# TensorE's order fixed in pieces through the memory heads and the S5 stage, with two float32 products of S5 dropped

## Chip, cores and metric

One core of one Trainium2 chip (trn2). The metric is the device time of one execution in microseconds; the time before is the median of three runs.

## What is computed

A decoder trunk of two layers over 1024 positions and 1024 channels, batch 1, float32. Layer 0 mixes tokens with a gated DeltaNet (GDN, 8 heads), layer 1 with an S5 state-space layer (64 groups of 16 channels, each driving one complex state of 64). Beside each mixer runs a cross-attention with 4 heads into 256 memory tokens. Cut to what matters here:

```python
def s5_scan(u, abar, bbar, c):                    # h_t = Abar h_{t-1} + Bbar u_t ; y_t = Re(C h_t)
    ...
    y = einsum('cbgp,gip->bcgi', st_re, c_re) - einsum('cbgp,gip->bcgi', st_im, c_im)

def s5_mixer(x, ...):
    u, xq = jnp.split(x @ w_in, [S5_DIM], axis=-1)
    y = s5_scan(u, ...) + d_skip * u
    zg = jax.nn.gelu(y)
    return zg * jax.nn.sigmoid(zg @ w_glu + b_glu), xq

def memory_attention(xq, mem, w_kv):
    k, v = jnp.split(mem @ w_kv, 2, axis=-1)
    s = einsum('blhd,bmhd->bhlm', q, k) * (XA_HEAD_DIM ** -0.5)
    return einsum('bhlm,bmhd->blhd', softmax(s), v)

for i in range(2):
    mix, xq = gdn_mixer(x, ...) if i == 0 else s5_mixer(x, ...)
    h = concat([mix, memory_attention(xq, mem, w_kv_mem[i])]) @ w_o[i]
    x = layer_norm(ALPHA * x + h, ...)
    x = layer_norm(ALPHA * x + square(relu(x @ mlp_w1[i])) @ mlp_w2[i], ...)
```

## The kernel before

**Arithmetic.** The large products run as three float32r matmuls each: an operand is split into a high and a low half (`load_split`: ScalarE casts the high half, VectorE subtracts to get the low one), and `mm3` (lines 115 to 117) adds high x high, high x low and low x high in one PSUM bank. `proj_half` is one 128-row projection of one half (512 positions): 8 blocks of three matmuls 128x512. Products of the S5 core and the chunk stage run in plain float32, which shows as two records a product. The activations of a layer stand in SBUF as `xT` (two halves, high and low).

**Order.** The kernel is written in program order, and the framework's planner then orders each engine's instructions: by priority in program order, by its own estimates of durations, and by when a rotating buffer becomes free. All engines then run their queues strictly in the order planned. `behind(mark)` adds edges without semaphores from each instruction traced inside it to a marked one on the same engine, so it only fixes order within an engine; before the change it serves only the S5 setup (`s5_side`).

**Buffers.** SBUF tags have fixed counts (`TAGS`: h1 7, h2 9, h3 7, h4 6, h5 5, w1 4, raw 2, xT 6), PSUM banks too (`BANKS`: mm 2, pa 3, pi 1, po 1, sc 1). Weight tiles come through the two `raw` buffers on SP's queue (SyncE issues most DMAs).

**Stages in order of time.** First the input and the keys of two GDN heads (`gdn_a`), the inverse of their small blocks on GpSimd (`gdn_inverse`), and the memory keys and values (`mem_kv`). Then the four memory heads (`attend`), the keys of a third GDN head between the first and the second. Then the chunk stage (`gdn_b`, eight heads), the output projection, the first MLP (`mlp`), beside which `s5_side` builds S5's tables: per core m of 8 and half b of 2, `s5_mats` forms H1 (and its ninth power H8), a Toeplitz source Z, G1 and H2, and stores them to HBM. Then the S5 stage, GLU, output projection and second MLP.

**`attend`** (lines 777 to 823) for one head: the query projection of both halves (tile `wq`), then per half two score tiles `sc` in the banks pi and pa, softmax (line 800 maximum, 804 exponential, 807 scaling), transposes `pT` (line 813) into po and sc, split, and the value product `pv`.

**`s5_core(m)`** (lines 1122 to 1174). SP loads u, the Toeplitz matrix M0 (from `zd`, one buffer for all cores) and per half G1, two tables `tab`, H1 and H2. G2 is G1 with its column halves swapped, by two ScalarE copies (1149, 1150). Four products G1 x u (line 1152) and four G2 x u (1154) give the drive and its partner; VectorE multiplies each by a table (1157, 1158), adds (1159), scans along the positions (1162) and makes r1 (1165), while GpSimd makes r2 (1166). The read-out adds for each group M0 x u (1169), H1 x r1 (1170) and H2 x r2 (1171) in one bank, then GELU (1173) and a store to `yd`. `s5_u(m)` is the projection (tile `wu`) that gives core m its input; it stands ahead of the core before it, and after odd cores comes one memory head. `glu` reads `yd` back, splits it and projects (tile `wg`).

Of the kernel before, what the change touches and what calls it, by code (L numbers as in the profile page):

```python
# [28 lines left out]
class Trunk:  # L29
    def __init__(self, ctx, tc, a):  # L30
        self.tc = tc
        self.nc = nc = tc.nc
        self.a = a
        self.uid = 0
        self.turn = 0
        self.proj = 0
        self.cp = ctx.enter_context(tc.tile_pool(name="cp", bufs=1))
# [22 lines left out]
    def behind(self, mark):  # L60
# [716 lines left out]
    def attend(self, src, xT, kv, h, permute, tag):  # L777

        nc = self.nc
        kh, kl, vh, vl = kv  # L780
        scale = P ** -0.5
        q = [None, None]

        def evac(hf, ps):
            hi = self.tile("h4", [P, HALF], F32R, "qh")
            lo = self.tile("h3", [P, HALF], F32R, "ql")
            nc.scalar.copy(hi, ps)
            nc.vector.tensor_tensor(lo, ps, f32(hi), op=ALU.subtract)
            q[hf] = (hi, lo)

        self.proj_fm(src, xT, evac, "wq")
        for hf in range(2):
            pp = []
            for c in range(2):
                ps = self.psum(("pi", "pa")[c], "sc", (P, 2, 256))
                for j in range(2):
                    t = slice((2 * c + j) * P, (2 * c + j + 1) * P)
                    self.mm3(ps[:, j, :], (q[hf][0][:, t], q[hf][1][:, t]), (kh[:, h, :], kl[:, h, :]), True, True)
                mx = self.tile("st", [P, 6], F32, "mx")
                nc.vector.tensor_reduce(mx[:, 0:2], ps, axis=AX.X, op=ALU.max)  # L800
                nc.vector.tensor_scalar(mx[:, 0:2], mx[:, 0:2], -scale, None, op0=ALU.mult)
                p = self.tile(tag, [P, 2, 256], F32, "p")
                for j in range(2):
                    nc.scalar.activation(p[:, j, :], ps[:, j, :], AF.Exp, bias=mx[:, j:j + 1], scale=scale, accum_out=mx[:, 2 + j:3 + j])
                nc.vector.reciprocal(mx[:, 4:6], mx[:, 2:4])
                for j in range(2):
                    nc.vector.tensor_scalar(p[:, j, :], p[:, j, :], mx[:, 4 + j:5 + j], None, op0=ALU.mult)
                pp.append(p)
            pt = []
            for m in range(2):  # L810
                ps = self.psum(("po", "sc")[m], "pT")
                for t in range(4):
                    nc.tensor.transpose(ps[:, t * P:(t + 1) * P], pp[t // 2][:, t % 2, m * P:(m + 1) * P], self.ident)
                hi = self.tile(tag, [P, HALF], F32R, "pTh")
                lo = self.tile(tag, [P, HALF], F32R, "pTl")
                nc.scalar.copy(hi, ps)
                nc.vector.tensor_tensor(lo, ps, f32(hi), op=ALU.subtract)
                pt.append((hi, lo))
            ps = self.psum("mm", "pv")
            d = slice(h * P, (h + 1) * P)  # L820
            for m in range(2):
                self.mm3(ps, (vh[:, m, d], vl[:, m, d]), pt[m], m == 0, m == 1)
            self.keep_rows(8 + h, hf, ps, permute)
# [69 lines left out]
    def s5_scratch(self):  # L893
# [3 lines left out]
        self.h2d = d("h2d", [8, P, 8, P])  # L897
# [143 lines left out]
    def combine(self, eng, x, y, pr, pi, op, b, nm, tag="h5"):  # L1041

        n = pr.shape[1]
# [6 lines left out]
        eng.tensor_tensor(o, o, w, op=op)  # L1050
        return o

    def s5_coeffs(self, m):
# [6 lines left out]
        co = self.tile("gb", [P, 6, 8, 16], F32, "co")  # L1060
        x = self.tile("h5", [P, 3, 8, 16], F32, "s5b")
        for o, n in ((x[:, 0], "b1"), (x[:, 1], "b2"), (co[:, 5], "c1"), (co[:, 3], "c2")):
# [4 lines left out]
        V.tensor_scalar(co[:, 2], co[:, 5], self.sg, -1.0, op0=M, op1=M)  # L1067
        V.tensor_scalar(co[:, 4], co[:, 3], self.sg, None, op0=M)
# [9 lines left out]
    def s5_mats(self, m, b, co):  # L1078
# [3 lines left out]
        A_, S_ = ALU.add, ALU.subtract  # L1082
# [3 lines left out]
        h1 = self.combine(V, co[:, 2], co[:, 3], re[:, 0:8, gl], im[:, 0:8, gl], A_, b, "H1")  # L1086
        nc.gpsimd.dma_start(self.h1d[m, :, gs, 0:8], h1)
        h8 = self.combine(V, co[:, 2], co[:, 3], re[:, 8:9, gl], im[:, 8:9, gl], A_, b, "H8", "S")
# [9 lines left out]
        g1 = self.combine(V, co[:, 0], co[:, 1], re[:, 0:8, gl], im[:, 0:8, gl], A_, b, "G1T")  # L1098
# [6 lines left out]
        h2 = self.combine(V, co[:, 4], co[:, 5], re[:, 1:9, gl], im[:, 1:9, gl], S_, b, "H2")  # L1105
        nc.gpsimd.dma_start(self.h2d[m, :, gs], h2.rearrange("p g e o -> p g (e o)"))
# [15 lines left out]
    def s5_core(self, m):  # L1122

        nc = self.nc
        V, G = nc.vector, nc.gpsimd
# [3 lines left out]
        M0 = self.s5t[:, T:2 * T].rearrange("p (g x) -> p g x", g=8)  # L1129
        z = self.zd[m]  # L1130
        nc.sync.dma_start(M0, bass.AP(z.tensor, z.offset, [[16, 8], [8 * 240, 16], [240, 8], [1, P]]))
        for b in range(2):
# [3 lines left out]
            def load(tag, nm, src):  # L1136
                t = self.tile(tag, [P, 4, P], F32, nm)
                nc.sync.dma_start(t, src)
# [5 lines left out]
            H2 = load("h2", "H2", self.h2d[m, :, gs])  # L1144

            p1 = self.psum("pa", "p1", (P, 4, P))
            p2 = self.psum("pa", "p2", (P, 4, P))
            G2 = self.tile("h1", [P, 4, P], F32, "G2")
            nc.scalar.copy(G2[:, :, 0:64], G1[:, :, 64:128])
            nc.scalar.copy(G2[:, :, 64:128], G1[:, :, 0:64])  # L1150
            for g in range(4):
                nc.tensor.matmul(p1[:, g, :], G1[:, g], u[:, 4 * b + g, :], start=True, stop=True)
            for g in range(4):
                nc.tensor.matmul(p2[:, g, :], G2[:, g], u[:, 4 * b + g, :], start=True, stop=True)
# [5 lines left out]
            w = self.tile("h3", [P, 4, P], F32, "wsc")  # L1160
            for g in range(4):
                V.tensor_tensor_scan(w[:, g, :], self.r8[:, g0 + g:g0 + g + 1].to_broadcast([P, P]), t1[:, g, :], 0.0, M, A_)
            r1 = self.tile("h1", [P, 4, P], F32, "r1")
            r2 = self.tile("h1", [P, 4, P], F32, "r2")
            V.tensor_tensor(r1, w, tab[0], op=M)
            G.tensor_tensor(r2, w, tab[1], op=M)
            py = self.psum("pi", "py", (P, 4, P))
            for g in range(4):
                nc.tensor.matmul(py[:, g, :], M0[:, 4 * b + g, :], u[:, 4 * b + g, :], start=True, stop=False)
                nc.tensor.matmul(py[:, g, 1:], H1[:, g], r1[:, g, 0:P - 1], start=False, stop=False)  # L1170
                nc.tensor.matmul(py[:, g, 1:], H2[:, g], r2[:, g, 0:P - 1], start=False, stop=True)  # L1171
            zg = self.tile("h3", [P, 4, P], F32, "zg")
            nc.scalar.activation(zg, py, AF.Gelu_apprx_tanh)
            nc.sync.dma_start(self.yd[m].rearrange("s (o g) n -> (s o) g n", o=16)[:, gs, :], zg)
# [9 lines left out]
    def glu(self):  # L1184
        nc = self.nc
        zT = self.new_xT()
# [8 lines left out]
        bg = self.const("bglu", [P, 8])  # L1195
        nc.sync.dma_start(bg, self.a["bglu"])
        for m in range(8):
            def evac(hf, ps):
                sg = self.tile("h3", [P, HALF], F32, "sig")
                nc.scalar.activation(sg, ps, AF.Sigmoid, bias=bg[:, m:m + 1])  # L1200
                z = self.tile("h4", [P, HALF], F32, "zz")
                nc.gpsimd.tensor_tensor(z, f32(zT[hf][0][:, m, :]), f32(zT[hf][1][:, m, :]), op=ALU.add)
                nc.vector.tensor_tensor(sg, sg, z, op=ALU.mult)
                nc.sync.dma_start(self.cat[m * P:(m + 1) * P, hf * HALF:(hf + 1) * HALF], sg)

            self.proj_fm(self.a["w_glu"][m], zT, evac, "wg")


    def run(self):
# [17 lines left out]
        att = lambda h: self.attend(a["w_in"][32 + h], xT, kv, h, True, "h2")  # L1227
# [4 lines left out]
        att(0)  # L1232
        keys_of(2)
        att(1)
        att(2)
        att(3)
# [25 lines left out]
        for m in range(8):  # L1262
            if 0 < m < 7:
                for _ in self.s5_u(m + 1, xT):
                    pass
            self.s5_core(m)
            if m % 2:
                self.attend(a["w_in5"][8 + m // 2], xT, kv, m // 2, False, "h5")
        self.glu()
# [130 lines left out]
```

## Time and profile before

| | us |
|---|---|
| median of 3 runs (3015.02 to 3018.07) | 3017.49 |
| profiled execution | 3012.86 |
| its span, first to last instruction | 3010.8 |
| memory heads of layer 0, 76.7 to 216.1 | 139.4 |
| chunk stage, 216.1 to 870 | 653.9 |
| S5 stage with heads and GLU, 1775 to 2165.2 | 390.2 |

A row of a table of stretches gives the stretch, its length, the busy time of each engine in it with the count of instructions, the granted TensorE clock (1.00 is full), the share of the DMA engines and GB/s. PE is TensorE's matmuls, PEld its weight loads, DVE VectorE, ACT ScalarE, POOL GpSimd; SPq is SyncE's queue. A row of waits reads "engine line waited for: us in total, times, longest". A row of groups reads line, engine, operation, output and inputs, shapes, count, busy us, mean ns, idle before and what ended it. Ends of matmuls are modelled, and consecutive ones overlap.

### The profile page before, as it was taken

To read this page: it belongs to the slowest core of one execution; us is meant where nothing else is said; L and a number is where in the kernel's file an instruction comes from. 1 tells how busy PE (TensorE), PEld (TensorE's weight loads), DVE (VectorE), ACT (ScalarE), POOL (GpSimd) and SP (SyncE) were. 2 spreads that over 40 slices of the span, in tenths; PEclk is the share of its full clock that TensorE was granted. 3 is DMA by queue.
4 is the path that set the end of the run, shared out by engine and by line. 5 is a ranking of instruction groups with operands and counts; after the bars stand their busy time and mean duration, and the time that the engine had idled before them with its cause. 6 is when DMAs were issued, how large, how long until landed. Compare 5 with 4: busy or idle time off the path is not lost. (4 is left out here: it accounts for less than half of the span.)

```text
span 3010.8 us, 36564 instructions
## 1 busy us (share of the span) xinstructions
PE 2832.7 (94%) x13629; PEld 2297.6 (76%) x13629; DVE 1765.6 (59%) x3491; ACT 964.1 (32%) x2069; POOL 517.2 (17%) x745
## 2 busy tenths in 40 slices
PE   8789888898999999999999998987999999999998
PEld 6668776676788888777777877775888888888887
DVE  7735667665679687666665644444378444444346
ACT  5334444453422322222222222223222222322221
POOL 3620543716002021211110101012002000000002
PEclk9889999999999999999999999997999999999999
DMA  5322433423532232322222165555341111111111
GB/s 196 108 60 78 107 110 102 111 95 83 173 97 69 72 100 86 100 81 83 76 91 79 71 205 166 168 150 168 109 133 44 63 42 50 49 49 49 50 50 56
DMA packets 197490, 288.12 MB, mean 96 GB/s; under 512 B 86032, under 2 KB 119008, under 8 KB 197312
## 3 DMA queue, kind: packets, MB, share of 16 engines
q1 hardware_dynamic: 181696, 245.46, 26.2%
q0 software_dynamic: 13312, 36.13, 3.8%
q10 hardware_dynamic: 2304, 4.20, 0.4%
q8 instruction: 107, 1.75, 0.2%
q14 instruction: 71, 0.58, 0.1%
HBM read 213.93 MB, written 71.79 MB: 95 GB/s over the span
## 5 line engine op out<-in xcount | busy, mean ns | idle before, releaser
L252 DVE TENSOR_TENSOR y<-tm,y 128x512 f32<-128x512 f32 x448 | 307.8, 689 | 197.5 <-PE tm L117 193.8
L115 PE MATMUL w<-xTh,w1h 128*128 128x512 f32 x1024 | 401.7, 393 | 0.1
L116 PE MATMUL w<-xTl,w1h 128*128 128x512 f32 x1024 | 400.7, 391 | 0.0
L117 PE MATMUL w<-xTh,w1l 128*128 128x512 f32 x1024 | 400.1, 391 | 0.0
L115 PE MATMUL tm<-w2h,hh 128*128 128x512 f32 x1024 | 399.1, 390 | 0.0
L116 PE MATMUL tm<-w2l,hh 128*128 128x512 f32 x1024 | 398.1, 389 | 0.0
L117 PE MATMUL tm<-w2h,hl 128*128 128x512 f32 x1024 | 397.3, 389 | 0.0
L107 ACT CAST w2h<-w2r 128x512 fp32r<-128x512 f32 x128 | 76.4, 622 | 556.9 <-PE tm L117 441.9
L176 POOL TENSOR_SCALAR mv<-mv 128x1 f32<-128x1 f32 x32 | 40.5, 1266 | 1165.9 <-DVE mv L175 1165.9
L117 PEld LDWEIGHTS w<-xTh,w1l 128*128 128x128 f32 x1024 | 192.8, 188 | 40.9 <-issue 0.8
L115 PEld LDWEIGHTS w<-xTh,w1h 128*128 128x128 f32 x1024 | 192.8, 188 | 40.7 <-ACT xTh L191 0.8
L115 PEld LDWEIGHTS tm<-w2h,hh 128*128 128x128 f32 x1024 | 192.3, 188 | 41.3 <-ACT hh L204 1.4
L116 PEld LDWEIGHTS w<-xTl,w1h 128*128 128x128 f32 x1024 | 192.9, 188 | 39.9 <-issue 0.4
L117 PEld LDWEIGHTS tm<-w2h,hl 128*128 128x128 f32 x1024 | 192.1, 188 | 40.2 <-DVE hl L205 0.3
L116 PEld LDWEIGHTS tm<-w2l,hh 128*128 128x128 f32 x1024 | 192.3, 188 | 39.6
L205 DVE TENSOR_TENSOR hl<-w,hh 128x512 fp32r<-128x512 f32 x128 | 87.2, 687 | 150.9 <-ACT hh L204 150.9
L95 DVE TENSOR_TENSOR w1l<-w1r,w1h 128x1024 fp32r<-128x1024 f32 x62 | 75.9, 1224 | 168.2 <-ACT w1h L94 168.2
L115 PE MATMUL wi<-xTh,wih 128*128 128x512 f32 x384 | 158.6, 413 | 2.3 <-ACT zc L679 2.3
L116 PE MATMUL wi<-xTl,wih 128*128 128x512 f32 x384 | 158.1, 412 | 0.0
L117 PE MATMUL wi<-xTh,wil 128*128 128x512 f32 x384 | 156.4, 407 | 0.0
L200 ACT ACTIVATE w<-w 128x512 f32<-128x512 f32 x128 | 74.5, 582 | 164.8 <-PE w L117 158.9
L94 ACT CAST w1h<-w1r 128x1024 fp32r<-128x1024 f32 x62 | 65.4, 1054 | 192.4 <-PE w L116 158.0
(416 smaller groups left out, 5783.3 us busy)
## 6 DMA issues: line engine op xcount, KB each, us to landing
w1r<-in_w_dram SPq DMA_DIRECT2D x64, 512.0 KB, 3.4
w2r<-in_w_dram SPq DMA_DIRECT2D x64, 512.0 KB, 3.5
wir<-in_w_in_dram SPq DMA_DIRECT2D x24, 512.0 KB, 3.6
wor<-in_w_o_dram SPq DMA_DIRECT2D x24, 512.0 KB, 3.5
cat<-cat SPq DMA_DIRECT2D x24, 512.0 KB, 3.2
gb<-gcd SPq DMA_DIRECT2D x32, 256.0 KB, 4.6
ntf<-nm POOLq DMA_DIRECT2D x32, 256.0 KB, 2.9
nm<-ntf SPq DMA_DIRECT2D x32, 256.0 KB, 3.0
```

The source lines that it names most:

```text
L94: nc.scalar.copy(hi, r)
L95: nc.vector.tensor_tensor(lo, r, f32(hi), op=ALU.subtract)
L107: nc.scalar.copy(hi, s)
L115: nc.tensor.matmul(ps, a[0], b[0], start=start, stop=False)
L116: nc.tensor.matmul(ps, a[0], b[1], start=False, stop=False)
L117: nc.tensor.matmul(ps, a[1], b[0], start=False, stop=stop)
L176: nc.gpsimd.tensor_scalar(mv[:, 2:3], mv[:, 1:2], 1e-5, None, op0=ALU.add)
L200: nc.scalar.activation(ps, ps, AF.Relu)
L205: nc.vector.tensor_tensor(lo, ps, f32(hi), op=ALU.subtract)
L252: nc.vector.tensor_tensor(o, ps, o, op=ALU.add)
```

## The change

- `piece()` puts every TensorE instruction traced inside it behind the last TensorE instruction of the piece before. Other engines' orders stay with the planner.
- `attend` is cut into `attend_q` (one query half at a time), `attend_s`, `attend_t` and `attend_v`. `memory_heads` lines these up for layer 0 so that query halves of the next head stand between scores, transposes and value products; the third key head (`last`) moves from behind the first head into the fourth.
- `s5_core` is cut into `s5_drive` and `s5_read`. The second drive product is replaced by a swap of row halves of the first one (two ScalarE copies), and r1, r2 with two read-out products by one r, which needs a second swap, one more VectorE product and a VectorE sum. G2, H2, its setup and its storage go; GpSimd computes nothing there. The loads of G1, tab, H1 and M0 move from SP's queue to GpSimd's; the two halves' read-outs use banks pi and po.
- `s5_front` lines up projections of the next core, heads and cores; cores 6 and 7 come after the last query projection.
- `glu` loads its first two weights and the bias before it reads `yd`; its first four outputs are begun with six of eight blocks, in three banks pa and one pi, and finished when the last two blocks are there.

```diff
+    @contextmanager
+    def piece(self):
+        with self.behind(self.pe):
+            yield
+        self.pe = {e: i for e, i in self.mark().items() if e == mybir.EngineType.PE}
...
@@ s5_mats
-        h2 = self.combine(V, co[:, 4], co[:, 5], re[:, 1:9, gl], im[:, 1:9, gl], S_, b, "H2")
-        nc.gpsimd.dma_start(self.h2d[m, :, gs], h2.rearrange("p g e o -> p g (e o)"))
...
@@ s5_core -> s5_drive, s5_read
             def load(tag, nm, src):
                 t = self.tile(tag, [P, 4, P], F32, nm)
-                nc.sync.dma_start(t, src)
+                nc.gpsimd.dma_start(t, src)
                 return t
...
+            def swap(o, x):
+                nc.scalar.copy(o[0:64], x[64:128])
+                nc.scalar.copy(o[64:128], x[0:64])
...
             for g in range(4):
                 nc.tensor.matmul(p1[:, g, :], G1[:, g], u[:, 4 * b + g, :], start=True, stop=True)
-            for g in range(4):
-                nc.tensor.matmul(p2[:, g, :], G2[:, g], u[:, 4 * b + g, :], start=True, stop=True)
+            swap(r, p1)
             V.tensor_tensor(t1, p1, tab[0], op=M)
-            V.tensor_tensor(t2, p2, tab[1], op=M)
+            V.tensor_tensor(t2, r, tab[1], op=M)
             V.tensor_tensor(t1, t1, t2, op=A_)
...
-            V.tensor_tensor(r1, w, tab[0], op=M)
-            G.tensor_tensor(r2, w, tab[1], op=M)
+            V.tensor_tensor(t1, t2, tab[1], op=M)
+            V.tensor_tensor(r, t2, tab[0], op=M)
+            swap(t2, t1)
+            V.tensor_tensor(r, r, t2, op=A_)
+            rs.append((r, H1))
...
-                nc.tensor.matmul(py[:, g, 1:], H1[:, g], r1[:, g, 0:P - 1], start=False, stop=False)
-                nc.tensor.matmul(py[:, g, 1:], H2[:, g], r2[:, g, 0:P - 1], start=False, stop=True)
+                nc.tensor.matmul(py[:, g, 1:], H1[:, g], r[:, g, 0:P - 1], start=False, stop=True)
...
@@ memory_heads (layer 0)
+        queries(0, 0)
+        queries(0, 1)
+        p = [scores(0, 0)]
+        for h in range(4):
+            if h == 0:
+                p.append(scores(0, 1))
+            if h < 3:
+                queries(h + 1, 0)
+            else:
+                last()
+            ta = attend_t(p[0])          # each step in a piece of its own
+            if h < 3:
+                queries(h + 1, 1)
+            tb = attend_t(p[1])
+            attend_v(ta, 0)
+            if h < 3:
+                p = [scores(h + 1, 0)]
+            attend_v(tb, 1)
+            if h < 3:
+                p.append(scores(h + 1, 1))
...
@@ s5_front: U projection of a core, Q S T V query, scores, transposes, values of head h, by halves
+        for m in range(6):
+            h = m // 2
+            if m % 2 == 0:
+                drive(m); U(m + 2, 0); U(m + 2, 1); read(m); Q(h, 0); Q(h, 1)
+            else:
+                S(h, 0); S(h, 1); drive(m); U(m + 2, 0); T(h, 0); U(m + 2, 1); T(h, 1); V(h, 0); read(m); V(h, 1)
+        Q(3, 0); Q(3, 1); drive(6); drive(7); S(3, 0); S(3, 1); read(6); read(7)
+        g = self.glu()
+        next(g)                          # bias, two weights, zT from yd
+        T(3, 0); next(g); T(3, 1); V(3, 0); next(g); V(3, 1)
+        for _ in g:
+            pass
```

More of the change, by code (lines that the diff above doesn't have):

```diff
@@ L775, in mem_kv, with attend_q @@
         return kh, kl, vh, vl
-    def attend(self, src, xT, kv, h, permute, tag):
+    def attend_q(self, src, xT, tags):
         nc = self.nc
[L780 to L786, printed above, removed]
+        w = self.load_split(src, "w1", "wq")
+        for hf in range(2):
+            ps = self.proj_half(w, xT, hf, "wq")
+            hi = self.tile(tags[0], [P, HALF], F32R, "qh")
+            lo = self.tile(tags[1], [P, HALF], F32R, "ql")
@@ L787, in evac @@
             nc.scalar.copy(hi, ps)
             nc.vector.tensor_tensor(lo, ps, f32(hi), op=ALU.subtract)
[L789 to L823, printed above, removed]
@@ new lines, in attend_t @@
+    def attend_t(self, pp, tags):
+        nc = self.nc
+        pt = []
+        for m in range(2):
+            ps = self.psum(("po", "sc")[m], "pT")
+            for t in range(4):
+                nc.tensor.transpose(ps[:, t * P:(t + 1) * P], pp[t // 2][:, t % 2, m * P:(m + 1) * P], self.ident)
+            hi = self.tile(tags[3], [P, HALF], F32R, "pTh")
+            lo = self.tile(tags[4], [P, HALF], F32R, "pTl")
+            nc.scalar.copy(hi, ps)
+            nc.vector.tensor_tensor(lo, ps, f32(hi), op=ALU.subtract)
+            pt.append((hi, lo))
+        return pt
@@ L825, in keep_rows, with attend_v @@
+    def attend_v(self, pt, kv, h, hf, permute):
+        vh, vl = kv[2:]
+        ps = self.psum("mm", "pv")
+        d = slice(h * P, (h + 1) * P)
+        for m in range(2):
+            self.mm3(ps, (vh[:, m, d], vl[:, m, d]), pt[m], m == 0, m == 1)
+        self.keep_rows(8 + h, hf, ps, permute)
     def keep_rows(self, k, hf, ps, permute):
@@ L1185, in glu @@
         nc = self.nc
+        bg = self.const("bglu", [P, 8])
+        nc.sync.dma_start(bg, self.a["bglu"])
+        ws = [self.load_split(self.a["w_glu"][m], "w1", "wg") for m in range(2)]
         zT = self.new_xT()
@@ L1194, in glu @@
                 nc.vector.tensor_tensor(zT[h][1][:, k, :], s, f32(zT[h][0][:, k, :]), op=ALU.subtract)
[L1195 to L1206, printed above, removed]
+        yield
@@ new lines, in evac, with part @@
+        def evac(m, hf, ps):
+            sg = self.tile("h3", [P, HALF], F32, "sig")
+            nc.scalar.activation(sg, ps, AF.Sigmoid, bias=bg[:, m:m + 1])
+            z = self.tile("h4", [P, HALF], F32, "zz")
+            nc.gpsimd.tensor_tensor(z, f32(zT[hf][0][:, m, :]), f32(zT[hf][1][:, m, :]), op=ALU.add)
+            nc.vector.tensor_tensor(sg, sg, z, op=ALU.mult)
+            nc.sync.dma_start(self.cat[m * P:(m + 1) * P, hf * HALF:(hf + 1) * HALF], sg)
+        def part(w, ps, hf, ks):
+            for k in ks:
+                c = slice(k * P, (k + 1) * P)
+                self.mm3(ps, (w[0][:, c], w[1][:, c]), (zT[hf][0][:, k, :], zT[hf][1][:, k, :]), k == 0, k == KT - 1)
@@ new lines, in glu @@
+        first = [(m, hf) for m in range(2) for hf in range(2)]
+        pss = []
+        for n, (m, hf) in enumerate(first):
+            pss.append(self.psum(("pa", "pa", "pa", "pi")[n], "wg"))
+            part(ws[m], pss[-1], hf, range(KT - 2))
+            if n < 2:
+                yield
+        for (m, hf), ps in zip(first, pss):
+            part(ws[m], ps, hf, range(KT - 2, KT))
+            evac(m, hf, ps)
+        for m in range(2, 8):
+            self.proj_fm(self.a["w_glu"][m], zT, lambda hf, ps: evac(m, hf, ps), "wg")
@@ new lines, in memory_heads, with queries, scores @@
+    def memory_heads(self, xT, kv, tags, last):
+        q = {}
+        banks = ("pi", "pa"), ("pa", "pa")
+        def queries(h, hf):
+            with self.piece():
+                if hf == 0:
+                    q[h] = self.attend_q(self.a["w_in"][32 + h], xT, tags), []
+                q[h][1].append(next(q[h][0]))
+        def scores(h, hf):
+            with self.piece():
+                return self.attend_s(q[h][1][hf], kv, h, tags, banks[hf])
+        queries(0, 0)
[8 more added lines that the diff above has]
+                last()
+            with self.piece():
+                ta = self.attend_t(p[0], tags)
+            if h < 3:
+                queries(h + 1, 1)
+            with self.piece():
+                tb = self.attend_t(p[1], tags)
+            with self.piece():
+                self.attend_v(ta, kv, h, 0, True)
+            if h < 3:
+                p = [scores(h + 1, 0)]
+            with self.piece():
+                self.attend_v(tb, kv, h, 1, True)
+            if h < 3:
+                p.append(scores(h + 1, 1))
@@ new lines, in s5_front, with U, Q, S @@
+    def s5_front(self, xT, kv):
+        tags = ("h4", "h4", "h5", "h4", "h5")
+        q, p, t, r = {}, {}, {}, {}
+        banks = ("pi", "pa"), ("pa", "pa")
+        def U(m, hf):
+            with self.piece():
+                if hf == 0:
+                    self.us[m % 2] = self.s5_u(m, xT)
+                next(self.us[m % 2])
+        def Q(h, hf):
+            with self.piece():
+                if hf == 0:
+                    q[h] = self.attend_q(self.a["w_in5"][8 + h], xT, tags), []
+                q[h][1].append(next(q[h][0]))
+        def S(h, hf):
+            with self.piece():
+                p[hf] = self.attend_s(q[h][1][hf], kv, h, tags, banks[hf])
+        def T(h, hf):
+            with self.piece():
+                t[hf] = self.attend_t(p[hf], tags)
+        def V(h, hf):
+            with self.piece():
+                self.attend_v(t[hf], kv, h, hf, False)
+        def drive(m):
+            with self.piece():
+                r[m] = self.s5_drive(m)
+        def read(m):
+            with self.piece():
+                self.s5_read(m, r.pop(m))
+        for m in range(6):
+            h = m // 2
+            if m % 2 == 0:
+                drive(m)
+                U(m + 2, 0)
+                U(m + 2, 1)
+                read(m)
+                Q(h, 0)
+                Q(h, 1)
+            else:
+                S(h, 0)
+                S(h, 1)
+                drive(m)
+                U(m + 2, 0)
+                T(h, 0)
+                U(m + 2, 1)
+                T(h, 1)
+                V(h, 0)
+                read(m)
+                V(h, 1)
+        Q(3, 0)
+        Q(3, 1)
+        drive(6)
+        drive(7)
+        S(3, 0)
+        S(3, 1)
+        read(6)
+        read(7)
+        g = self.glu()
+        next(g)
+        T(3, 0)
+        with self.piece():
+            next(g)
+        T(3, 1)
+        V(3, 0)
+        with self.piece():
+            next(g)
+        V(3, 1)
+        for _ in g:
+            pass
@@ L1261, in run @@
         kv = self.mem_kv(1)
[L1262 to L1269, printed above, removed]
+        self.s5_front(xT, kv)
         y = self.quad(F32, "y") + self.quad(F32, "y")
```

83 lines of the change are left out of this document (50 added, 33 removed).

## Prediction

> **What bounds the kernel now.** I read the page's head first, then a table of stretches by stage, then TensorE's waits in the two stages that the diff rewrites, then single rows for rates.
>
> ```profile
> span 3010.8 us, 36564 instructions
> PE 2832.7 (94%) x13629; PEld 2297.6 (76%) x13629; DVE 1765.6 (59%) x3491; ACT 964.1 (32%) x2069; POOL 517.2 (17%) x745
> ```
> ```profile
> core 0: us, PE busy (x) PEld busy (x) DVE busy (x) ACT busy (x) POOL busy (x), PEclk, DMA share, GB/s
> 76.70:216.10 139.40, 113.40 (x479) 87.44 (x478) 78.85 (x178) 53.66 (x140) 65.45 (x105) 0.80 0.32 87
> 216.10:870.00 653.90, 592.55 (x3216) 473.90 (x3215) 417.21 (x919) 290.43 (x841) 217.06 (x299) 0.98 0.36 106
> ...
> 2061.40:2074.60 13.20, 0.03 (x1) 0.04 (x1) 3.93 (x7) 4.94 (x8) 0.00 (x0) 0.63 0.91 305
> ```
> ```profile
> 1775.00:2165.20 390.20, 338.50 (x1760) 279.82 (x1760) 156.42 (x293) 115.19 (x225) 46.56 (x32) 0.94 0.52 159
> 2165.20:2300.00 134.80, 134.53 (x613) 110.58 (x614) 112.14 (x170) 33.05 (x57) 11.63 (x13) 1.00 0.28 92
> ```
> TensorE is the bound: after 2165.2 it runs without gaps at clock 1.00. Two stages fall short of that: the memory heads of the first layer (76.7 to 216.1, clock 0.80), and S5 with its heads and the GLU (1775 to 2165.2, clock 0.94), with a hole of 13.2 us. No other engine is full in them. What ends TensorE's waits, in the heads and then in the S5 stage:
>
> ```profile
> PE pT L813 <- DVE p L807: 14.5, 12, 3.6
> PE sc L115 <- ACT p L804: 3.7, 4, 1.4
> ```
> ```profile
> PE wg L115 <- ACT wgh L94: 13.2, 1, 13.2
> PE py L1169 <- DMA s5t<-zd: 8.8, 4, 4.0
> PE sc L115 <- ACT p L804: 7.6, 4, 3.4
> PE py L1171 <- POOL r L1166: 6.4, 10, 0.6
> PE pT L813 <- DVE p L807: 5.0, 7, 2.2
> ```
> The reader sees short chains through other engines (softmax, scan, loads) that TensorE sits out, because no long projection stands in the gap.
>
> **What the stages' work takes at full clock.** Matmuls overlap, so a rate is the distance between starts. The first fence is the chain of waits inside the S5 stage, the second its timeline, the third the counts:
>
> ```profile
> 1944.45 0.22 PE py L1169 x2
> ...
> 1947.62 9.52 DMA s5t<-zd
> ...
> 1957.73 0.23 PE wq L115
> ```
> ```profile
> 1977.49 0.28 PE L116 MATMUL sc<-kv,qh 128*128 128x256 f32 x1
> 1977.61 0.28 PE L117 MATMUL sc<-kv,ql 128*128 128x256 f32 x1
> ```
> ```profile
> L117 PE MATMUL wg<-xTh,wgl 128*128 128x512 f32 x128 | 50.4, 394 | 0.0
> L117 PE MATMUL wu<-xTh,wul 128*128 128x512 f32 x96 | 37.8, 394 | 0.5 <-DVE wul L95 0.5
> ...
> L116 PE MATMUL wq<-xTl,wqh 128*128 128x512 f32 x64 | 26.5, 414 | 0.0
> ...
> L1170 PE MATMUL py<-r,H 128*128 128x127 f32 x128 | 26.0, 285 | 3.9 <-DVE r L1165 3.9
> L1154 PE MATMUL p<-s5t,G 128*128 128x128 f32 x128 | 17.5, 275 | 0.0
> ...
> L813 PE MATMUL pT<-ident,p 128*128 128x128 f32 x64 | 11.9, 317 | 5.0 <-DVE p L807 5.0
> L115 PE MATMUL sc<-kv,qh 128*128 128x256 f32 x32 | 10.1, 315 | 7.6 <-ACT p L804 7.6
> ```
> So a 512-wide matmul takes 0.227, a 256-wide one 0.12, a float32 product of 128 two records and 0.223 together (0.111 a record).
> S5 stage: three matmuls each, so 3 x (128 wg + 96 wu + 64 wq) = 864, with 48 pv and 48 mv 960, x 0.227 = 218; sc 96 x 0.12 = 11.5; five groups of 128 records (two p, three py) and 64 pT, 704 x 0.111 = 78. Together 307 of 390 us: 83 are lost, more than the 51.7 idle.
> Heads stage: 192 wq, 48 pv and the 48 of the third key head, 288 x 0.227 = 65.4; 96 sc 11.5; about 96 records 10.7. Together 87.5 of 139.4: 52 are lost, 26 of them idle.
>
> By the busy rows alone the idle time is all that order can win. The Trainium skill, "Trainium Kernel Development and Optimization", section "Performance Expectations", calls matmul busy time a bad metric for the distance to the roofline, since matmuls are pipelined. The trace agrees: 113.4 us busy for 87.5 us of work. The busy reading is priced among the rivals.
>
> **The change, part by part.**
> *Dropped products.* L1154 and L1171 go: 2 x 128 x 0.111 = 28.5 us of TensorE, all in its own queue, so all on the path. 307 becomes 279.
>
> *What replaces them.* Half-swaps on ScalarE and one more chain on VectorE. Rows for it:
> ```profile
> 1805.52 1.37 DVE L1162 TENSOR_TENSOR_SCAN wsc<-r,t 128x128 f32<-128x128 f32 x4
> 1806.92 0.69 DVE L1165 TENSOR_TENSOR r<-wsc,tab 128x512 f32<-128x512 f32 x1
> ```
> ```profile
> L1113 ACT COPY s5t<-wu 128x512 f32<-128x512 f32 x12 | 7.0, 585 | 24.6 <-PE wu L117 22.6 <-DMA wqr<-in_w_in_dram 2.0
> ```
> Per half core VectorE goes from 4 x 0.69 + 1.37 = 4.1 to 6 x 0.69 + 1.37 = 5.5 us; ScalarE gets four swap copies and loses two G copies; POOL loses its product. A swap of 64 rows is not in the trace; between 0.40 (a 256-wide G copy) and 0.59 (512 wide, above) I take 0.59, the same width. Sixteen halves add 22 us to VectorE's 156 and about 25 to ScalarE's 115: still below 60% of a 330 us stage, so hidden. The latency is what counts: product 0.9, swap 1.2, three passes 2.1, scan 1.4, two passes 1.4, swap 1.2, sum 0.7, about 9 with handovers for the first half and 14 for the second.
>
> *Cover, even cores.* Between `drive` and the second half of `read` stand 1.8 of drive, two projections of 24 x 0.227 = 5.4 each, and 2.7 of read: 15.3 against 14. I take 1 us of stall each, 3 in all (bounds 0 and 4 each). M0 must wait for the read before it (one buffer) and landed in 9.52 us; 14 us stand before its use.
> *Odd cores.* Three of a head's four score tiles and two drive products share the three "pa" banks, so drive waits for exponentials:
> ```profile
> L804 ACT ACTIVATE p<-sc,mx 128x256 f32<-128x256 f32 x32 | 14.9, 478 | 3.1 <-DVE mx L801 3.0
> ```
> Six of a head's eight at 0.48, with their sums' read-outs, and the first maximum make 5.5 us or so after the first score against 3.7 of TensorE work. I take 3 us each, 9 in all (bounds 0 and 6 each).
> *Start.* Value weights and first tables as now: 9 us (5 to 12).
> *Tail.* Cores 6 and 7 come with no projection left. VectorE needs 4 x 5.5 for them and some 6 for the last softmax, 28 us, beside 13.6 us of TensorE work: 14 to 15 missing, with GELU and bank waits 18 (bounds 10 and 28). The GLU then starts on six of eight blocks (72 matmuls, 16 us, and 5 of attention). Store and load of core 7 with casts are at most two times the 9.52 of M0's load, which has the same size, and 3: covered but for 1 us at worst. The GLU's weights are loaded ahead, so the 13.2 hole goes. Late next is that last scan.
> *Clock and type changes.* 12 us: 5 after the tail's gaps, 7 at switches.
> Sum: 279 + 3 + 9 + 9 + 18 + 12 = 330; 60 us won (40 to 85).
>
> *Loads moved to POOL.* Nine per core leave SP, where they queue ahead of weights, and all are issued by POOL:
> ```profile
> SPq L1138 <- POOL r L1166: 44.0, 13, 5.3
> ```
> ```profile
> L1087 POOL DMA_DIRECT2D h1d<-H x16 | 12.4, 773 | 243.4 <-DVE cw L1049 237.2 <-DVE H L1050 6.2
> ```
> 72 x 0.77 = 55 us on a POOL that is busy 46.6 of 390: hidden. Behind a waiting M0 stand only the next core's tables, wanted a core later. I count zero (up to 2 us a core if M0 is late).
>
> *Memory heads.* Per head TensorE has 18.3 us (60 matmuls of 0.227, 24 of 0.12, 16 transposes), and VectorE's 78.9 for the whole stage stays below 87.5. A projection half of 5.4 us stands between scores and transposes; it covers a softmax of about 5 us (two tiles' maxima and scalings at about 0.7, four exponentials at 0.48 with read-outs). Left are 1 us a head before the second value product, 5 at the last head, whose only filler is the third key head, 3 of switches: 87.5 + 12 = 99.5, 40 won. The key head's VectorE work now meets the first `gdn_b`; I take 5 back (0 to 15). Net 35 (20 to 47).
>
> *Setup in the first MLP.* The H2 tables go (three VectorE passes and a store per half core), which shortens this wait:
> ```profile
> PE pz L1093 <- DVE H L1050: 7.4, 8, 1.8
> ```
> 4 us won (0 to 7), the queue behind H being shorter. The chunk stage between 216 and 870 is replanned by the shift, either sign, 8 us; counted at zero.
>
> Sum: 60 + 35 + 4 = 99, rounded to 100. The profiled execution took 3012.86 (span 3010.8 and 2.1 around it); it becomes 2913. The median shown, 3017.49, lies 4.6 above it, so half of that is added: 2915.
>
> **The rivals.**
> Nearly everything closes: tail 10 and odd stalls near 0 give 85 in S5, the heads 47, the setup 6: 138, so 2878. For it: projections are plentiful. Against: the pa banks and the bare tail.
> The busy reading holds: half rate in these stages stays whatever the order, and only idle time shrinks. Heads 26 - 12 = 14; S5 51.7 + 28.5 - 51 = 29; setup 4: 47, so 2970. For it: VectorE in the heads is already at 78.9 of what would be 99. Against: the clock is 1.00 wherever TensorE is dense.
> Nothing but the drop: the planner still orders the other engines, and a wrong order there lets the fixed pieces wait as long as now: 28.5, so 2989.
> Slower: M0 through POOL. TensorE may no longer step past a read, so each late M0 is paid in full. It now lands 9.5 us after its release and may take 14 unseen; it decides at 14 + 100/8, about 26 us, and at 30 the time is 3017 - 100 + 8 x 16 = 3045. The Trainium skill, "DMA: Bandwidth & Descriptors", gives the software path 1 us to the first byte against 0.6; by that alone 8 cores would pay at most 3 us. No row here shows that load on POOL.
>
> **How the numbers follow.** Chances: my sum 0.60 (its own range 2893 to 2938), nearly everything 0.17, busy reading 0.13, drop only 0.06, slower 0.04. The range 2872 to 2962 takes in the first two and the edge of the third. Within 0.2% (6 us, what this measurement tells from no change) needs the drop to be eaten by new stalls: 0.02; slower by more 0.04; faster 0.94.
>
> **What would show it.** Right: no L1154 or second read-out rows; the S5 stage near 330 us and the heads near 100, both at clock 0.95 or more except a dip between the last query projection and the GLU; waits of drive on exponentials. Wrong: read-outs waiting on the load of M0; `pT` still waiting on VectorE; a chunk stage longer than 654 us.

## The result, and the profile after

The changed kernel took 2931.13 us (median of 4 runs, 2924.60 to 2936.22) against 3017.78 for the kernel before (4 runs, 3015.02 to 3021.89): ratio 0.9711, 95% interval 0.9688 to 0.9733. The forecast was 2915 with a range of 2872 to 2962: inside, and 16 us above the number. The profiled execution took 2924.60 (span 2922.9), at the lower end of the runs.

The head of the page, after:

```profile
span 2922.9 us, 35948 instructions
PE 2769.2 (95%) x13373; PEld 2261.3 (77%) x13373; DVE 1752.8 (60%) x3467; ACT 994.0 (34%) x2104; POOL 536.4 (18%) x785
```

256 TensorE instructions are gone, 128 of each dropped product. VectorE has not become busier, since the H2 tables that it no longer builds outweigh the new chain in S5; POOL has 19 us more: its issues of loads outweigh the products that it lost.

The table of stretches, after: memory heads with the third key head, chunk stage, first MLP with the S5 setup, S5 with its heads and the GLU.

```profile
core 0: us, PE busy (x) PEld busy (x) DVE busy (x) ACT busy (x) POOL busy (x), PEclk, DMA share, GB/s
78.49:170.30 91.81, 87.94 (x466) 73.83 (x465) 65.40 (x155) 48.55 (x124) 53.50 (x86) 1.00 0.36 92
170.30:833.30 663.00, 595.90 (x3229) 476.13 (x3228) 431.25 (x941) 294.01 (x856) 231.66 (x318) 0.97 0.37 110
935.10:1719.10 784.00, 781.89 (x3664) 632.71 (x3663) 497.42 (x1157) 221.68 (x366) 115.19 (x201) 1.00 0.27 86
1721.50:2076.70 355.20, 301.62 (x1504) 255.72 (x1504) 174.79 (x325) 147.45 (x262) 69.78 (x85) 0.92 0.53 163
```

One stretch of before that the prediction did not show, for the first MLP:

```profile
971.90:1771.60 799.70, 788.02 (x3665) 634.60 (x3663) 529.42 (x1213) 222.19 (x368) 121.78 (x214) 1.00 0.27 89
```

| stage | before | after | won | forecast |
|---|---|---|---|---|
| memory heads | 139.4 | 91.8 | 47.6 | 40 |
| chunk stage | 653.9 | 663.0 | -9.1 | -5 |
| first MLP, S5 setup | 799.7 | 784.0 | 15.7 | 4 |
| S5, heads, GLU | 390.2 | 355.2 | 35.0 | 60 |

Together 89.2, of 87.9 between the two spans. The heads run at clock 1.00 instead of 0.80. In S5 the clock is 0.92 and 54 us are idle, and TensorE's waits there say why:

```profile
PE p L1166 <- DMA G<-g1d: 34.6, 4, 10.5
PE p L1166 <- ACT p L813: 6.5, 3, 2.2
PE py L1195 <- ACT p L813: 4.9, 1, 4.9
PE py L1195 <- ACT zg L1198: 2.3, 2, 1.8
PE mv L123 <- ACT wvh L102: 2.2, 1, 2.2
PE mv L124 <- DVE wvl L103: 2.0, 3, 0.8
PE pT L827 <- DVE pTl L831: 1.4, 1, 1.4
```

The last six rows were in the sum, and no larger than there. The first was not: four times the drive stands at its second half, because G1 of that half has not landed. POOL's timeline at the second of them (core 2), then TensorE's:

```profile
1797.04 0.54 POOL L1151 DMA_DIRECT2D tab<-tabd  x1 [5.83 <-PE py L1196]
1798.60 1.34 POOL L1185 DMA_DIRECT2D s5t<-zd  x1 [1.02 <-PE py L1196]
1799.93 0.79 POOL L1151 DMA_DIRECT2D H<-h1d  x1
1800.72 1.09 POOL L1151 DMA_DIRECT2D G<-g1d  x2
```
```profile
1799.76 1.05 PE L1166 MATMUL p<-s5t,G 128*128 128x128 f32 x8
1809.12 2.08 PE L1166 MATMUL p<-s5t,G 128*128 128x128 f32 x8 [8.30 <-DMA G<-g1d]
```

Read it from the top. POOL stands at a table of core 3 until the read-out of core 1 frees its buffer (5.83 us on `PE py`), then issues M0 (`s5t<-zd`), H1, and only then G1 of core 2's second half together with G1 of core 3. The drive of core 2 has begun at 1799.76, one value product after read 1, so it meets a load issued at 1800.72. That load lands late too; the issue tables, before and then after (the last number is the median from issue to landing):

```profile
G<-g1d SPq DMA_DIRECT2D x16, 256.0 KB, 3.4
```
```profile
G<-g1d POOLq DMA_DIRECT2D x16, 256.0 KB, 10.0
s5t<-zd POOLq DMA_DIRECT2D x8, 512.0 KB, 10.7
```

Nothing in these rows made G1 wait but its place: it is issued right behind H1 with no wait of its own, while the table (5.83 us) and M0 (1.02 us) ahead of it waited for read 1. That it could have gone a whole core earlier is what `g1_pair_first` shows below.

### The profile page after: what moved, and what is told of

Read it like the earlier page. It is cut to its first block, busy times and chain, and to the rows that moved or that the text cites. A ratio compares the mean times of both kernels' runs of the same rounds, so it can differ in the third digit from the quotient of the medians.

```text
span 2922.9 us, 35948 instructions
## 1 busy us (share of the span) xinstructions
PE 2769.2 (95%) x13373; PEld 2261.3 (77%) x13373; DVE 1752.8 (60%) x3467; ACT 994.0 (34%) x2104; POOL 536.4 (18%) x785
```

## The experiments

The kernels share the program ahead of the S5 stage, but for `keep_h2` and `keys_early`, and without the edges the planner also orders the memory heads a little differently. "S5" is the stretch from the first value projection of the second layer's memory (`mv`) to the first product of its output projection (`tm`), in the one profile of each kernel; the last column is TensorE's wait for G1 in it. Even between kernels whose program is alike up to S5, the start of S5 varies from 1721.5 to 1731.9 us, so a few us are read from the S5 column rather than from the medians.

| kernel | median, us | ratio to before, interval | S5 | G1 waits |
|---|---|---|---|---|
| the change | 2931.13 | 0.9711 (0.9688 to 0.9733) | 355.2 | 34.6 |
| g1_on_sp | 2941.48 | 0.9746 (0.9728 to 0.9763) | 365.8 | 38.7 |
| m0_on_sp | 2920.58 | 0.9678 (0.9663 to 0.9694) | 345.7 | 23.5 |
| loads_on_sp | 2928.51 | 0.9703 (0.9687 to 0.9720) | 352.8 | 32.3 |
| g1_pair_first | 2896.71 | 0.9602 (0.9588 to 0.9616) | 324.4 | none |
| no_pieces | 2906.82 | 0.9634 (0.9618 to 0.9649) | 332.2 | 16.9 |
| g1_first_free | 2883.71 | 0.9561 (0.9547 to 0.9575) | 312.8 | 0.5 |
| tail_order | 2896.40 | 0.9604 (0.9588 to 0.9620) | 320.4 | 3.8 |
| tail_free | 2882.88 | 0.9559 (0.9543 to 0.9576) | 307.1 | 5.5 |
| tail_free_m0_sp | 2881.48 | 0.9552 (0.9535 to 0.9568) | 308.4 | none |
| double_products | 2950.66 | 0.9780 (0.9765 to 0.9795) | 374.7 | 31.7 |
| keep_h2 | 2945.74 | 0.9766 (0.9746 to 0.9785) | 359.3 | 26.0 |
| keys_early | 2936.93 | 0.9741 (0.9725 to 0.9757) | 358.0 | 26.9 |

**Which queue, or which place in it.** Three kernels move loads back to SP: G1 alone, M0 alone, all nine of a core.

```diff
g1_on_sp:     G1 = load(...)                ->  nc.sync.dma_start(G1, self.g1d[m, :, gs])
m0_on_sp:     nc.gpsimd.dma_start(M0, ...)  ->  nc.sync.dma_start(M0, ...)
loads_on_sp:  both, and load() itself through nc.sync
```

> The changed kernel with the loads of G1 issued by SP instead of POOL; all else as in the change. Theory: the 34.6 us that TensorE waits for G1 in cores 2, 4, 7 and at the start come from G1's place in POOL's queue, behind a table load that waits for the read-out before and behind M0. On SP these waits go (under 3 us left), and with them some 5 us of lowered clock: S5 stage from 355 to about 318 us, time about 2895. Rival one: VectorE's chain is late anyway, so the read-outs (py) wait in place of the drive: S5 stage above 345, time 2920 or more. Rival two: SP's queue is as late as POOL's (it waits long for u's store): G1 is still waited for 20 us or more, time 2915 to 2940.

> The changed kernel with the load of M0 issued by SP instead of POOL; G1 stays on POOL. Theory (place in POOL's queue, behind a table load that waits for the read-out before): G1 is issued only about 1.3 us earlier but lands some 4 us after issue instead of 8 to 10, without M0's 512 KB ahead of it: the waits for G1 go from 34.6 to about 15 us, time about 2910. Rival (it is M0's bulk alone that makes G1 late): the waits go under 5 us and the time equals that with G1 on SP, about 2895. Second rival: M0 on SP is late for its read-outs (py waits on zd 8 us or more, as before the change), time 2925 or more.

> Edit: all nine loads of a core (G1, tables, H1, M0) go through SP, as in the kernel before; pieces and order stay. Theory (what counts is whether a G1 stands behind something that waits, on either queue): SP has waits of its own (u and y stores behind casts and GELUs), so no gain over 8 us: 2923 to 2945, waits of `p` on G1 20 us or more. Rival (the move to POOL is what costs): the waits fall below 10 us, and the time to 2900 to 2910.

TensorE's first row of waits in S5, in this order:

```profile
PE p L1167 <- DMA G<-g1d: 38.7, 6, 9.6
```
```profile
PE p L1166 <- DMA G<-g1d: 23.5, 4, 6.3
```
```profile
PE p L1166 <- DMA G<-g1d: 32.3, 8, 7.3
```

G1 on SP is later still (2941.48, just past the range of its second rival), although it lands 4.4 us after its issue: SP has waits of its own, in this stage 122.9 us for the copies that make u and 25.6 us for the GELUs behind y. Everything on SP equals the change within the intervals. So it is not the move from one queue to the other that costs. M0 away from POOL takes about 10 us off the medians, half of what its theory expected, and G1, still through POOL, lands in 6.7 us instead of 10.0: the 512 KB ahead of it in its own queue were part of its delay. The load of u, now in one queue with M0, lands in 8.9 us instead of 5.2, and `drive(7)` waits 3.0 us for it. The Trainium skill, "Trainium Kernel Development and Optimization", section "Key Constraints", says that DMAs issued from SP, ACT and POOL run on the same 16 engines and interleave, so that several issuers save only the issue time. The landing times here differ: which queue the bulk stands in moved G1's landing by 3.3 us.

**The place itself.** Both halves' G1 are requested at the head of `s5_drive`; POOL and the pieces stay. In POOL's order the pair of the next core then stands behind the read's M0 and H1, where G1 of this core's second half stood: a whole core ahead of its use.

```diff
+        G1s = [load("h1", "G1", self.g1d[m, :, 4 * b:4 * b + 4]) for b in range(2)]
         for b in range(2):
-            G1 = load("h1", "G1", self.g1d[m, :, gs])
+            G1 = G1s[b]
```

> Edit: both halves' G1 are requested at the head of s5_drive, ahead of tables and H1, still through POOL; the pieces stay. In the planned order the pair of core m+1 then stands where G1 of core m's second half and of core m+1's first half stood, so the second half's G1 is requested a core earlier. Theory (place in the queue: behind M0 and the H1 that wait for the read before): the waits of `p` on G1 fall from 34.6 us to under 10 (the first core's 5.4 may stay) and the time from 2931 to about 2903 (2896 to 2912), as the clock recovers too. Rival (the data of G1 lands slowly through POOL, 10 us after its issue, wherever it stands): more than 20 us of waits stay, 2918 to 2935.

TensorE's waits in S5, and the stretch:

```profile
PE py L1196 <- ACT p L813: 8.9, 1, 8.9
PE p L1167 <- ACT p L813: 6.5, 3, 2.2
PE sc L123 <- DVE t L1172: 4.7, 1, 4.7
PE py L1196 <- ACT zg L1199: 2.4, 1, 2.4
PE sc L123 <- ACT t L1162: 2.1, 1, 2.1
PE mv L123 <- ACT wvh L102: 1.9, 2, 1.2
```
```profile
1726.90:2051.30 324.40, 293.91 (x1505) 250.29 (x1505) 174.41 (x325) 143.93 (x260) 69.25 (x84) 0.96 0.58 179
```

The row of G1 is gone, the median falls by 34.4 us, and S5 is 31 us shorter. One half of the rival's claim is true: G1 still takes long to land, 9.8 us after its issue. It no longer matters, since nobody wants it yet. This is the cause of the 25 us by which S5 missed its forecast, shown by moving one request.

**The edges.** `piece` yields without adding edges; the program's order, and with it the planner's priorities, stay. First on the change, then with the G1 pair first.

```diff
     def piece(self):
-        with self.behind(self.pe):
-            yield
-        self.pe = {e: i for e, i in self.mark().items() if e == mybir.EngineType.PE}
+        yield
```

> The changed kernel, same program order, same arithmetic, but without the edges between pieces: the planner orders TensorE by its own estimates. Theory (the fixed order carries the gain of the heads and much of S5's): heads stage back above 115 us (92 in the change), S5 above 365 us, time 2955 to 2975. Rival (program order and the dropped products are enough, the edges add nothing): heads 92 to 97 us, time within 8 us of 2931. Second rival (the planner fills the waits for G1 by itself): heads as in the change or somewhat longer, S5 below 345, time under 2922.

> Edit: as g1_pair_first, and piece() adds no edges (the planner may move products past each other; the program's order is the same). Without the pair first, dropping the edges won 24 us. Theory (the edges cost only where TensorE stands at a late G1, which nothing may step past): with G1 early the two versions lie within 8 us of each other, this one near 2898 (2890 to 2905). Rival (the edges cost by themselves, in the tail above all): this one is 16 us or more below g1_pair_first, near 2885.

Waits for G1 in `no_pieces`, then what is left in `g1_first_free` (the first three rows):

```profile
PE p L1164 <- DMA G<-g1d: 16.9, 4, 8.1
```
```profile
PE py L1194 <- ACT p L811: 8.8, 1, 8.8
PE sc L121 <- DVE t L1170: 4.7, 1, 4.7
PE mv L122 <- DVE wvl L101: 1.9, 3, 0.8
```

Without edges the change is 24 us faster, as the second rival had it; the theory that the edges carry the gain fell. Half of the G1 waits close, because products of the next core's projection step into them. With G1 early the edges still cost 13.0 us. That lies between the 8 and the 16 of the two expectations, so neither is confirmed whole. The trace has 11.6 of it in S5: the 6.5 us of waits of `p` on exponentials are filled (a few `wu` matmuls stand between the scores and the drive), 3.1 us come from the tail between the first drive product of core 6 and the dense GLU (52.8 to 49.7 us), and 2 are not tied to a row. In the memory heads the edges change nothing that the trace shows: the same stages run from 79.1 to about 172 without them, from 78.5 to 170.3 with them.

**The tail.** On `g1_pair_first`, on `g1_first_free`, and on the latter with M0 on SP:

```diff
-        Q(3, 0); Q(3, 1); drive(6); drive(7); S(3, 0); S(3, 1); read(6); read(7)
+        drive(6); Q(3, 0); drive(7); Q(3, 1); read(6); S(3, 0); S(3, 1); read(7)
```

> Edit: on g1_pair_first (2896.7 us; pieces kept), the tail of S5 stands as drive(6), Q(3,0), drive(7), Q(3,1), read(6), S(3,0), S(3,1), read(7), so the last head's two query projections (10.8 us) stand behind the drives instead of before them. In g1_pair_first TensorE idles 18.9 us there (8.9 for the scores' bank before read 6, 4.75 and 2.1 for drive 7's banks, 2.4 for a GELU). Theory (these waits are the price of a tail without cover; the prediction put 18 on it): 8 to 13 us of them go, 2885 (2881 to 2890). Rival (VectorE's 28 us for the two scans and the last softmax set the tail's end whatever the order): under 4 us won, 2893 to 2897, with the wait moved to read 7 or to the transposes.

> Edit: the same tail on g1_first_free (2883.7 us; no edges), where 8.8 + 4.7 + 1.8 us of these waits are left. Theory: 6 to 12 us less, 2875 (2871 to 2879), the fastest version so far. Rival (VectorE sets it): 2880 to 2885.

> Edit: tail_free (2882.9 us: no edges, G1 pair first, query projections between the last drives) with M0 loaded through SP. In tail_free drive(7) waits 5.5 us for its G1, which POOL issues behind M0 of core 6. Theory (M0 ahead of it in POOL's queue is what makes that G1 late): the wait falls under 2 us and S5 from 307 to about 303, 2878 (2873 to 2882). Rival (G1 of core 7 is late because its request stands behind the table and the H1 that wait for read 5, M0 or no M0): the wait stays at 4 us or more, 2881 to 2887.

TensorE's waits in S5 in `tail_order`, then the first row of `tail_free_m0_sp`:

```profile
PE p L1167 <- ACT p L813: 6.5, 3, 2.2
PE wg L123 <- ACT xTh L1222: 4.0, 3, 2.8
PE p L1167 <- DMA G<-g1d: 3.8, 1, 3.8
PE py L1197 <- DVE r L1181: 3.0, 2, 2.6
```
```profile
PE p L1165 <- DMA s5t<-ud: 7.0, 1, 7.0
```

The theory fell, twice: the 8.9 + 4.7 are gone, but the median is the same within the spread of the runs, and S5 is 4 to 6 us shorter where 8 to 13 and 6 to 12 were expected. The waits moved: `drive(7)` is reached before its G1 has landed, read 7 waits for its scan, and the GLU for the casts of the last y. With M0 on SP the wait for G1 goes as its theory had it, and `drive(7)` waits 7.0 us for its u instead, which now stands beside M0 on SP as in `m0_on_sp`. Neither expectation had that. In `tail_free` the chain that ended last runs through the last scan, the softmax, the GELU and the casts of y; that this chain ends the S5 stage whatever covers its first part is likely, and not shown. The three kernels without edges and with the G1 pair first (2881.5 to 2883.7 us) cannot be told apart; the change takes 1.7% longer than they do.

**The dropped products.** Each drive product and each product with M0 is issued twice, the second over the first: as many records more as the change dropped, in the change's own order.

```diff
+                for _ in range(2):
                     nc.tensor.matmul(p1[:, g, :], G1[:, g], u[...], start=True, stop=True)
...
+                nc.tensor.matmul(py[:, g, :], M0[...], u[...], start=True, stop=True)
                 nc.tensor.matmul(py[:, g, :], M0[...], u[...], start=True, stop=False)
```

> Edit: each drive product and each product with M0 is issued twice, the second writing over the first: 2 x 128 records more on TensorE, as many as the change dropped, with nothing else moved. Theory (the prediction's sum, 0.111 us a record, all on the path): 28 us more than the change, 2959 (2953 to 2965). Rival (part of them falls into waits, since TensorE waits for G1 and exponentials right there): 10 to 20 us more, 2941 to 2951.

```profile
PE p L1167 <- DMA G<-g1d: 31.7, 4, 9.1
```

19.5 us, so the rival holds: about a third of the 28.5 falls into time in which TensorE would have waited. Two places show it. Around cores 6 and 7 the tail grows by 3.2 us (51.6 to 54.8 from the first drive product of core 6 to the dense GLU) for 64 records, 7.1 us by the sum; and the waits for G1, in the row above, shrink by 2.9, of which 1.4 lie in that tail.

**The setup.** H2 is built and stored again as before the change, and read by nobody.

```diff
+        V.tensor_scalar(co[:, 5], co[:, 3], self.sg, None, op0=M)
...
+        h2 = self.combine(co[:, 5], co[:, 4], re[:, 1:9, gl], im[:, 1:9, gl], b, "H2", op=ALU.subtract)
+        nc.gpsimd.dma_start(self.h2d[m, :, gs], h2.rearrange("p g e o -> p g (e o)"))
```

> The changed kernel with the setup of H2 put back into the first MLP (six coefficient tiles, three VectorE passes and a store per half core); H2 is stored and not used. Theory: the dropped H2 passes give the 16 us that the stage between 935 and 1707 became shorter by: the waits of pz on VectorE return to 7 us or more, time about 2945. Rival: that stage won by a better plan and not by H2: the time stays within 5 us of 2931.

The first MLP's stretch, and TensorE's waits in it:

```profile
936.60:1736.00 799.40, 789.47 (x3664) 635.59 (x3663) 529.31 (x1213) 221.80 (x367) 123.71 (x217) 0.99 0.27 89
```
```profile
PE pz L1112 <- DVE H L1070: 5.5, 7, 1.5
PE pg L1120 <- DVE G1T L1070: 2.2, 1, 2.2
PE pg L1120 <- ACT z L1115: 0.7, 1, 0.7
```

799.4, as before the change (799.7); in the kernels without H2 this stretch is 783.4 to 785.5. The time rises by 14.6. So H2's setup, three VectorE passes and a store per half core and a coefficient per core, costs 15 us. The waits explain 7 of them: those that end on H, G1T or z are 8.4 us here against 1.1 us in the change. The rest is TensorE's busy time, 789.5 against 781.9 with the same count, and most of that is the granted clock. It is 1.00 in the change's whole stretch; here it falls to half for 3.4 us behind the wait that ends at 1215.6:

```profile
1217.90:1221.30 3.40, 3.40 (x10) 2.62 (x9) 0.87 (x2) 0.23 (x1) 0.54 (x1) 0.50 0.04 10
```

The same happens from 1269.1 and from 1422.7, also beside such waits. Three times 3.4 us at half clock cost 5.1 us of work; the other 2.5 are not tied to a row.

**The give-back after the heads.** The third key head stands ahead of the memory heads instead of inside the last one.

```diff
-        self.memory_heads(xT, kv, tags, lambda: keys_of(2))
+        keys_of(2)
+        self.memory_heads(xT, kv, tags, lambda: None)
```

> Edit: on the change itself, the third key head (48 projections and its convolution on VectorE) stands ahead of the memory heads instead of inside the last of them. In the change the chunk stage behind the heads takes 663.0 us against 653.9 before. Theory (the prediction's: the key head's VectorE work meets the first gdn_b, which costs the 9 us given back): the chunk stage returns to 656 or less, the last memory head gains about 5 us of waits for its softmax, and the sum is 2927 (2922 to 2932). Rival (the give-back is a replanned chunk stage or its clock, not the key head's place): the chunk stage stays at 660 or more, and the time goes to 2934 to 2940.

Stretches of `keys_early` (the key head with the memory heads, and the chunk stage up to the last transposed output), then the second one of the change:

```profile
77.00:187.00 110.00, 96.92 (x482) 80.62 (x481) 83.22 (x180) 53.48 (x141) 65.54 (x105) 0.94 0.41 109
187.00:855.00 668.00, 602.30 (x3264) 481.08 (x3263) 426.18 (x941) 294.24 (x854) 217.92 (x299) 0.97 0.36 105
```
```profile
170.30:843.00 672.70, 605.59 (x3274) 483.65 (x3272) 439.60 (x964) 297.89 (x870) 231.66 (x318) 0.97 0.37 110
```

In the change the chunk stage holds 13.4 us more of VectorE's work and 13.7 more of POOL's than in `keys_early`, which is the key head's. Moving it out shortens the stage by 4.7 us, about half of what was given back and between the two expectations, and costs 16.8 us in front of it (108.6 against 91.8 from the first product of the key head or the first query to the first of `gdn_b`), where 5 were expected: TensorE's waits there are 13.0 us against 3.7, the longest 4.0 for a bank held by the first softmax, and the clock is 0.94 against 1.00. The time does not fall: the median is 5.8 us above the change's. That the displaced key head is half of the give-back is likely but not settled. From its first product to its last output transposes the stage takes 667.7 us here, less than in any of the twelve profiles with the key head inside the memory heads, but those vary by 8 us among themselves (672.2 to 680.6).

`keep_h2` and `keys_early` also have less wait for G1 than the change (26.0 and 26.9 us) mostly by its name: the wait of core 7, 10.5 us under G1's name in the change, stands there under VectorE's (9.7 and 10.2 us). At core 7 both are late.

## Why the prediction was right, and where not

*Sign and size.* 100 us were forecast on the profiled execution and 88.3 came (3012.86 to 2924.60); by the medians 86.7. That the total came within 16 us is partly luck: S5 won 25 us less than forecast, while the heads won 7.6 and the setup 11.7 more. The mechanism held in the heads: where TensorE's order fills the gaps, the work runs at its rate by starts. The heads took 91.8 us for 87.5 us of work, which puts the busy reading (14 us to be won there) aside.

*The step that failed* is "Loads moved to POOL": "Behind a waiting M0 stand only the next core's tables, wanted a core later. I count zero". G1 of the same core's second half stood there too. It measured 34.6 us of waits, against a bound of 2 us a core "if M0 is late", 16 in all. Nor was it POOL's queue alone: with all nine loads on SP in the new order TensorE waited 32.3 us for G1. What the sum left out is where G1 stands among the requests, on either queue, with a fixed order that lets TensorE do nothing else meanwhile. Moving the request ahead won 31 us in S5 and 34.4 of the time. With it the stage takes 324.4, and the forecast's 330 is met within 6.

The rest of that sum, in `g1_pair_first`: even cores 1 (3 forecast), odd cores 6.5 (9), the tail 4.7 + 2.1 + 8.9 + 2.4 + 0.7 = 18.8 (18). With the start's 3.6 (9) and the 279 of work that makes 309; 15 remain for clock and type changes (12). In the change the tail's waits were 18.3 as well, 10.5 of them under G1's name. So 24.1 of the 34.6 came on top. The projections behind these three waits lost 4.2 to the clock (last section) and the four drive products ahead of those projections 2.5 (1.7 us each time instead of 0.9): together 30.8, as much as moving the request won there.

*Slower by M0.* It did not come: no read-out waited for M0, though it landed 10.7 us after its issue. What was feared of M0 happened to the load behind it. The first-byte times of the Trainium skill ("DMA: Bandwidth & Descriptors", section "Specifications") are about 1 us on the software path against about 0.6; no row here isolates that latency. The tables landed in 3.1 us through POOL and in 4.3 through SP before, so the path as such was not slow; the place in it was.

*Dropped products.* 28.5 were counted as all on the path; put back into the change they cost 19.5. In a stage with 54 us of idle time, work beside the waits was partly free, and so, it follows, was its removal.

*Memory heads.* 47.6 won against 40, since the 12 us of remaining stalls and switches were 3.7 us of waits:

```profile
PE pT L827 <- DVE pTl L831: 1.8, 2, 1.2
PE pv L123 <- DVE ql L794: 1.7, 1, 1.7
PE pv L124 <- DVE pTl L831: 0.2, 1, 0.2
```

The give-back was 9 against 5. A chunk stage over 654 us had been named as a sign of being wrong, though the sum's own 5 us made it 659; it came at 663.0. Net 38.5 against 35 in the profile; over the kernels that are alike there, heads and chunk stage up to the start of its last output transposes take 764.0 to 774.4 us against 802.5 before, so 28 to 38.

*Setup.* 15.7 against 4, outside its bounds of 0 to 7. The bound was the 7.4 us of the one row of waits shown. `keep_h2` shows what it left out: the waits of `pg` (2.2 and 0.7), and 7 us or so of TensorE's own busy time, most of it a lowered clock behind the waits.

*The hole at the GLU* (13.2 us) is gone as forecast. The clock in S5 did not come up as forecast: it is 0.92 instead of 0.95 or more, and with the pair first, without the waits for G1, it is 0.96.

*Not foreseen at all:* that the fixed edges themselves cost. The edges take 24 us of the gain back in this form, and 13 where the loads are early. What brings the gain is then the order of the program, the dropped work and the GLU's early weights; the dropped products were worth 19.5 us and H2's setup 14.6 by the runs that put them back, and no run takes the order or the early weights out alone. The fastest kernels here, near 2882 us (ratio 0.955 to 0.956), have the order without the edges.

## What to carry to other kernels

When a load changes its queue, list what stands in the new queue between an instruction that waits and the loads behind it, and for each of those when its reader wants it; a load that waits for nothing itself can be held up for as long as the one ahead of it, and a fixed order on the reader's side then pays the wait in full. Give the planner an order by priority first and pin it with edges only where the trace shows that it goes wrong. Removed work is worth its full time only where the engine has no waits beside it, and on a stage whose neighbours it delays it can be worth more than its own waits show.

## What was not expected of the hardware

The same 256 KB load landed 3.4 us after its issue on SP before, 10.0 on POOL behind 512 KB of M0, and 6.7 on POOL with M0 on SP. After a wait for G1 the granted clock stays low for a while, as a table of stretches of the change shows: each first row is the 48 projection matmuls behind a wait (5.4 and 10.4 us), each second one the next 48:

```profile
1744.00:1757.00 13.00, 13.00 (x51) 10.56 (x50) 7.41 (x14) 4.28 (x8) 2.37 (x4) 0.84 0.26 86
1760.40:1771.50 11.10, 11.10 (x52) 9.21 (x51) 0.69 (x1) 1.28 (x3) 3.22 (x4) 1.00 1.02 255
...
1879.00:1891.20 12.20, 12.20 (x52) 10.01 (x52) 5.93 (x11) 4.39 (x8) 1.30 (x2) 0.90 0.14 44
1894.60:1905.60 11.00, 11.00 (x51) 9.12 (x51) 0.69 (x1) 1.29 (x3) 3.21 (x4) 1.00 1.03 260
```

By the starts, the 48 behind the three waits in cores 0, 2 and 4 took 13.0, 12.1 and 12.1 us instead of 11.0 each, 4.2 in all; the clock was 0.84 to 0.91 there. The shortest of these waits (5.4 us) cost the most. In the first MLP of `keep_h2` waits of 1.0 to 2.2 us came with 3.4 us at half clock three times; another of 1.0 us there, and the one of 1.1 us in the change, came without.
